# Three small moves in the middle of a hybrid attention layer: a k copy on ScalarE, two key norms, and one step of a GELU given to GpSimd

## The chip, the cores and the metric

The kernel runs on one core of a Trainium2 chip. The metric is the device time of one execution in microseconds (us), the median of several runs. TensorE does the matmuls, VectorE (DVE), ScalarE (ACT) and GpSimd (POOL) the work on tiles, and DMA queues the traffic with the chip's memory.

## The reference, cut to what matters

```python
h = rms_norm(x, norm_w)                      # x: 512 tokens of 1024
q_a, k_a, v_a, z_a, q_b, kc, vc, ksl, vsl, kwn, vwn, gate_b, z_b, gate_m = split(h @ w_in)
# mixer A: 8 heads of 64, causal attention over blocks of 256 keys
o_a = moba(rms_norm(heads(q_a)), rms_norm(heads(k_a)), heads(v_a), bias_a)
# mixer B: a compressed, a selected and a window branch
k_cmp = rms_norm(compress(kc)); v_cmp = compress(vc)     # compress: gelu(win @ w1) @ w2
o_b = nsa(rms_norm(heads(q_b)), k_cmp, v_cmp, rms_norm(ksl), vsl, rms_norm(kwn), vwn, gate_b, bias_b)
merged = sigmoid(g1) * ((o_a * silu(z_a)) @ w_a) + sigmoid(g2) * ((o_b * silu(z_b)) @ w_b)
out = x + merged @ w_out
```

All numbers are float32. With 512 tokens the block choices of both mixers take in every past block, so the attention is dense and causal.

## The kernel before, in words

**Precision.** A float32 matmul is done as three faster ones: each operand is split into a high part (`wh`, `hh`, `ks`) and a low part (`wl`, `hl`, `kx`), and high by high, high by low and low by high are summed in PSUM (`mm3`, L375 to L389). Weights come by DMA in 128x512 tiles `wr`; the high part is a cast on ScalarE or GpSimd (L352, L356), the low part a subtraction on VectorE or GpSimd (L361).

**Order.** Everything is written by Python generators: the projections (`gemms`), the attention units (`attention`), the two compressions (`cmp`). A planner in the kernel keeps an estimated clock `now` and an estimated end of work for each engine (`free`), draws the next piece of matmul work, and runs chains of small operations (`Chain`, L171 to L250) from a heap ordered by estimated time. A step of a chain names the engines that may do it, with a cost; the planner takes the engine that would be done first. What comes out is a fixed order of instructions on each engine. An engine works through its own order strictly, so an instruction that waits holds up those behind it. `Chain(t).call(fn)` runs `fn` when the planner's clock reaches `t`, and costs the planner nothing.

**Attention.** An attention unit is one head. Its scores come in four blocks of 128 queries, the longest first: `sps` = q by `ks` (L1033) and by `kx` (L1034), then on VectorE `sb` (scores and bias, L1052), on ScalarE the exponential `P` (L1067), on VectorE the reciprocal of the sum `sst` (L1070), on GpSimd the scaling of `P` (L1071). One unit later TensorE transposes `P` into `pt` (L1080), ScalarE and VectorE split it into `ph` (L1092) and `pl` (L1094), and TensorE multiplies by v into `O` (L1114). The first transposes of a unit need all four blocks of `P`, the 128x128 one being scaled last.

**k of mixer A** (`k_pair`, L978). Two heads are transposed at once into `pq` (L956). For each, ScalarE casts the high part twice, into the upper and the lower 64 partitions of `ks` (L987); VectorE writes the low part into the upper 64 partitions of `kx` (L989); ScalarE copies that into the lower 64 (L992), after the low parts of both heads. The matmul with `kx` needs both halves.

**k of mixer B** (`norm`, L714, called for the four token tiles of `kb` with `gi` 4). ScalarE takes the projection out of PSUM into `nraw` (L723) and squares it (L725); VectorE sums the squares into `nss` (L726) and scales the sum (L426); GpSimd raises it to the power -1/2, `nr` (L427); two products on VectorE or GpSimd follow (L728, L734). The tiles are read far later, when mixer B's heads begin. The norms of `qb` run through the same function.

**Compression** (`compress_h`, L855), once for k and once for v. After the first matrix `hps` and a small sum `pu` (L878) comes the GELU: ScalarE makes the square and a copy `u` (L885, L886), GpSimd two steps on `gt` (L888, L889), ScalarE the tanh (L890), VectorE the last step (L891: `gt` = (`gt` + 1) by `u`). For k, TensorE goes on with `pk` (L905); for v, VectorE first spreads `gt` into `Gv` (L896).

Of the kernel before, what the change touches and what calls it, by code (L numbers as in the profile page):

```python
# [25 lines left out]
EPS = 1e-6  # L26
# [80 lines left out]
def hybrid_kernel(ctx: ExitStack, tc: tile.TileContext, x, x0, xT, wtok, wchan, wz, wgate, gains, w1,  # L107
                  relone, wbr, wout, consts, out):
    nc = tc.nc
# [19 lines left out]
    now = [0.0]  # L129
# [267 lines left out]
    mhalf = cp.tile([P, 8], F32, name="mhalf")  # L397
# [6 lines left out]
    gn = cp.tile([P, 6, DH], F32, name="gn")  # L404
# [16 lines left out]
    pos = cview("pos").rearrange("p (k i) -> p k i", k=2)  # L421
    w2t = cview("w2").rearrange("p (k a d) -> p k a d", k=2, a=2)

    def rsqrt_mean(c, dst, ss, n, w, parts=P):
        v = (lambda z: z() if callable(z) else z)
        c.do({"D": 70}, lambda e: e.tensor_scalar(v(ss), v(ss), 1.0 / n, EPS, op0=ALU.mult, op1=ALU.add))  # L426
        c.do({"p": 430 + POWC * w}, lambda e: e.tensor_tensor(v(dst), v(ss), mhalf[:parts, :w], op=ALU.pow))  # L427

    def att(name, dt=F32R):
        return ap_.tile([P, 512], dt, name=nm(name), tag="a")  # L430
# [283 lines left out]
    def norm(ch, dst, ps, t, H, gi):  # L714

        b, n = {}, H * DH
        out = dst.bitcast(F32)[:, :n].rearrange("p (h d) -> p h d", d=DH)

        def f0(e):
            b["t"] = alloc("nraw", "nraw", (P, 8, DH))  # L720
            b["raw"] = b["t"][:, :H]
            b["ss"], b["r"] = (sp.tile([P, 8], F32, name=nm(z), tag=z, bufs=4)[:, :H] for z in ("nss", "nr"))
            e.activation(b["raw"], ps[:, :n].rearrange("p (h d) -> p h d", d=DH), AF.Copy, scale=rx[:, t:t + 1])  # L723
        ch.do({"A": 100 + cap(n)}, f0, ps, "nraw")
        ch.do({"A": ca(n)}, lambda e: e.activation(out, b["raw"], AF.Square))  # L725
        ch.do({"D": cd(n)}, lambda e: e.reduce_sum(b["ss"], out, axis=AX.X))  # L726
        rsqrt_mean(ch, lambda: b["r"], lambda: b["ss"], DH, H)
        ch.do(either(n), lambda e: e.tensor_mul(out, b["raw"], b["r"].unsqueeze(2).to_broadcast([P, H, DH])), lambda: b["t"])  # L728
        if gi == 1:
            z = out[:, 4:]  # L730
            ch.do(either(256), lambda e: e.tensor_mul(z, z, gn[:, 1, :].unsqueeze(1).to_broadcast([P, 4, DH])))
        elif gi:
            z = out.rearrange("p (a b) d -> p a b d", a=2)
            ch.do(either(256), lambda e: e.tensor_mul(z, z, gn[:, gi:gi + 2, :].unsqueeze(2).to_broadcast([P, 2, 2, DH])))  # L734

    def hl4(t):
        return t.rearrange("p (h s d) -> p h s d", s=2, d=DH)
# [117 lines left out]
    def compress_h(kv):  # L855
        yield need(f"xw{kv}")
        st = xws[kv]
        yield room("t")
        hps = psum("t", "hps")
        for q in range(8):  # L860
            ws = W1.take(1, 256)
            if W1.i == 1:
                W1.bufs, W.bufs = W1B, NRAW - W1B
            for i in range(2):
                yield ws[i][2].ready
                c = 2 * q + i
# [12 lines left out]
        yield 300
        t1 = sp.tile([P, P], F32, name=nm("gt"), tag="c2")  # L880
        u = sp.tile([P, P], F32, name=nm("u"), tag="u", bufs=1)
        ch = Chain(now[0] + 230)

        def square(e):
            e.activation(t1, ub[:, :P], AF.Square)  # L885
            e.copy(u, ub[:, :P])  # L886
        ch.do({"A": 160}, square)
        ch.do({"D": 200}, lambda e: nc.gpsimd.tensor_scalar(t1, t1, 0.044715, 1.0, op0=ALU.mult, op1=ALU.add))  # L888
        ch.do({"D": 200}, lambda e: nc.gpsimd.tensor_mul(t1, t1, u))  # L889
        ch.do({"A": 200}, lambda e: e.activation(t1, t1, AF.Tanh, scale=0.7978845608028654))  # L890
        ch.do({"D": 200}, lambda e: e.scalar_tensor_tensor(t1, t1, 1.0, u, op0=ALU.add, op1=ALU.mult), ub)  # L891
        G = t1
        if kv:
            yield room("gmt")
            G = alloc("gmt", "Gv", (P, 4, 4, C32))
            ch.do({"D": 600}, lambda e: e.tensor_copy(  # L896
                G, t1.rearrange("p (q c) -> p q c", c=C32).unsqueeze(2).to_broadcast([P, 4, 4, C32])))
        yield ch.ready
        yield from (compress_v2 if kv else compress_k2)(G)
# [75 lines left out]
                 pt if r else None)  # L975
            box.append((z, c))

    def k_pair(boxes, name, col, firsts=None):  # L978

        yield room("t")  # L980
        pt = turn(name, col)
        yield 4 * 109
        c = Chain(now[0] + 230)
        kk = [(att("ks"), att("kx")) for _ in range(2)]
        for r, (ks, kx) in enumerate(kk):
            for i in range(2):
                c.do({"A": 478}, lambda e, r=r, z=ks[64 * i:64 * i + 64, :]: e.copy(z, pt[64 * r:64 * r + 64, :]))  # L987
        for r, (ks, kx) in enumerate(kk):
            c.do({"D": 602}, lambda e, r=r, ks=ks, kx=kx: e.tensor_sub(  # L989
                kx[0:64, :], pt[64 * r:64 * r + 64, :], ks[0:64, :].bitcast(F32)), pt if r else None)  # L990
        for r, (ks, kx) in enumerate(kk):
            c.do({"A": ca(512)}, lambda e, kx=kx: e.copy(kx[64:128, :], kx[0:64, :].bitcast(F32)))  # L992
# [850 lines left out]
```

## Time and profile before

| | us |
|---|---|
| runs shown | 450.40, 452.17, 452.28 |
| their median | 452.17 |
| the profiled execution | 451.19 |
| its span, first to last instruction | 449.4 |
| TensorE busy in the span | 442.5 (98%) |
| VectorE busy | 381.7 (85%) |
| ScalarE busy | 302.9 (67%) |
| GpSimd busy | 202.6 (45%) |

The profiled execution is one of its own, 0.98 below the median of the runs; 1.8 of its time lie outside the span. The granted TensorE clock is 1.0 throughout. A row of the timeline has the start in us, the duration in us, the engine, the line, the operation and its tiles; in brackets stands the idle time of the engine before it and who ended it. `x3` is three equal instructions in a row.

### The profile page before, as it was taken

To read this page: it belongs to the slowest core of one execution; us is meant where nothing else is said; L and a number is where in the kernel's file an instruction comes from. 1 tells how busy PE (TensorE), PEld (TensorE's weight loads), DVE (VectorE), ACT (ScalarE), POOL (GpSimd) and SP (SyncE) were. 2 spreads that over 40 slices of the span, in tenths; PEclk is the share of its full clock that TensorE was granted. 3 is DMA by queue.
4 is the path that set the end of the run, shared out by engine and by line. 5 is a ranking of instruction groups with operands and counts; after the bars stand their busy time and mean duration, and the time that the engine had idled before them with its cause. 6 is when DMAs were issued, how large, how long until landed. Compare 5 with 4: busy or idle time off the path is not lost.

```text
span 449.4 us, 8537 instructions
## 1 busy us (share of the span) xinstructions
PE 442.5 (98%) x2779; PEld 395.2 (88%) x2779; DVE 381.7 (85%) x934; ACT 302.9 (67%) x713; POOL 202.6 (45%) x238
## 2 busy tenths in 40 slices
PE   8999999999999999999999999999999999999997
PEld 7888888899788998888999999989988999998886
DVE  5999899789997797788899999877967699999783
ACT  6866778867988797476878677687764355454460
POOL 1243337866784573176675554764760221311000
PEclk9999999999999999999999999999999999999999
DMA  7885746877975979959978867976667888889872
GB/s 254 293 274 187 243 146 201 212 220 185 272 196 161 220 220 249 298 146 226 278 200 223 212 175 185 253 203 157 196 182 171 230 244 235 258 232 290 279 240 95
DMA packets 55085, 98.21 MB, mean 219 GB/s; under 512 B 5312, under 2 KB 9536, under 8 KB 55040
## 3 DMA queue, kind: packets, MB, share of 16 engines
q1 hardware_dynamic: 39808, 68.30, 47.5%
q0 software_dynamic: 7616, 14.68, 20.1%
q10 hardware_dynamic: 7616, 14.68, 9.9%
q8 instruction: 22, 0.36, 0.3%
q14 instruction: 23, 0.19, 0.1%
HBM read 90.69 MB, written 36.31 MB: 283 GB/s over the span
## 4 chain that ended last, share of the span: by engine, by line
PE 80%; DVE 9%; ACT 5%; DMA 3%; issue 2%; SPq 0%; ACTq 0%; DVEq 0%
PE pgw L386 17%; PE pgt L386 14%; PE pbr L386 10%; PE po L386 9%; PE pgc L386 7%; PE O L1114 5%; PE pgf L680 5%; PE pt L1080 5%; PE sps L1033 3%; PE sps L1034 3%; DMA T<-rtab 1%; DMA wr<-in_w 1%; ACT ks L987 1%; DVE sb L1052 1%; DVE pl L1094 1%
## 5 line engine op out<-in xcount | busy, mean ns | idle before, releaser
L361 DVE TENSOR_TENSOR wl<-wr,wh 128x512 fp32r<-128x512 f32 (+1 forms) x150 | 101.9, 696 | 2.7 <-ACT wh L352 2.1
L352 ACT CAST wh<-wr 128x512 fp32r<-128x512 f32 (+1 forms) x130 | 77.0, 608 | 16.2 <-DMA wr<-wsum 5.4
L356 POOL TENSOR_SCALAR wh<-wr 128x512 fp32r<-128x512 f32 (+1 forms) x39 | 31.5, 819 | 78.4 <-DVE wl L361 24.3
L1071 POOL TENSOR_SCALAR P<-P,sst,gate 128x512 f32<-128x512 f32 (+3 forms) x56 | 46.3, 830 | 40.0 <-DVE sst L1070 32.0
L1067 ACT ACTIVATE P<-sb,sst 128x512 f32<-128x512 f32 (+3 forms) x88 | 50.8, 577 | 16.5 <-DVE sst L1052 15.2
L1052 DVE CUSTOM_DVE_ANT_0 sb<-sps,T 128x512 f32<-128x512 f32 (+3 forms) x96 | 46.0, 483 | 15.3 <-PE sps L1034 13.0
L386 PE MATMUL pgt<-wh,hh 128*128 128x512 f32 (+2 forms) x160 | 56.6, 354 | 0.0
L386 PE MATMUL pgt<-wl,hh 128*128 128x512 f32 (+2 forms) x160 | 55.8, 348 | 0.0
L386 PE MATMUL pgt<-wh,hl 128*128 128x512 f32 (+2 forms) x160 | 55.7, 348 | 0.0
L386 PE MATMUL pgw<-th,wh 128*128 128x256 f32 x240 | 48.9, 281 | 0.4 <-DVE gm L1528 0.4
L1092 ACT CAST ph<-pt 128x512 fp32r<-128x512 f32 (+2 forms) x72 | 33.8, 476 | 19.7 <-PE pt L1080 18.4
L386 PE MATMUL pgw<-hh,wh 128*128 128x256 f32 x160 | 45.2, 282 | 0.3 <-ACT c L1469 0.2
L386 PE MATMUL pgw<-hh,wl 128*128 128x256 f32 x160 | 44.4, 278 | 0.0
L386 PE MATMUL pgw<-hl,wh 128*128 128x256 f32 x160 | 44.4, 277 | 0.0
L1080 PE MATMUL pt<-cst,P 128*128 128x128 f32 x232 | 40.7, 272 | 0.4 <-DVE pl L1094 0.3
L386 PEld LDWEIGHTS pgw<-th,wh 128*128 128x128 f32 x240 | 39.4, 188 | 1.2 <-DVE gm L1528 0.8
L1094 DVE TENSOR_TENSOR pl<-pt,ph 128x512 fp32r<-128x512 f32 (+2 forms) x72 | 38.6, 548 | 1.6 <-ACT ph L1092 1.3
L427 POOL TENSOR_TENSOR nr<-nss,mhalf 128x8 f32<-128x8 f32 (+1 forms) x16 | 26.9, 1680 | 20.5 <-DVE nss L426 18.8
L386 PEld LDWEIGHTS pgt<-wl,hh 128*128 128x128 f32 x160 | 30.1, 188 | 4.1 <-DVE wl L361 0.2
L386 PE MATMUL pgw<-th,wl 128*128 128x256 f32 x120 | 33.3, 277 | 0.0
L386 PEld LDWEIGHTS pgt<-wh,hh 128*128 128x128 f32 x160 | 30.1, 188 | 3.4 <-ACT nraw L723 0.2
L386 PEld LDWEIGHTS pgt<-wh,hl 128*128 128x128 f32 x160 | 30.1, 188 | 3.2
(272 smaller groups left out, 1292.3 us busy)
## 6 DMA issues: line engine op xcount, KB each, us to landing
wr<-wsum SPq DMA_DIRECT2D x56, 256.0 KB, 4.0
wr<-in_wtok SPq DMA_DIRECT2D x36, 256.0 KB, 4.9
wsum<-in_wgate ACTq DMA_DIRECT2D x16, 512.0 KB, 5.0
wsum<-wsum POOLq DMA_DIRECT2D x14, 512.0 KB, 7.5
wr<-in_wgate SPq DMA_DIRECT2D x24, 256.0 KB, 4.7
xsum<-th SPq DMA_DIRECT2D x16, 256.0 KB, 2.6
T<-rtab SPq DMA_DIRECT2D x16, 256.0 KB, 5.3
wr<-in_w SPq DMA_DIRECT2D x16, 256.0 KB, 3.8
```

The costliest lines, as they stand in the source:

```text
L352: e.copy(hi, raw)
L356: e.tensor_scalar(hi, raw, 1.0, 1.0, op0=ALU.mult, op1=ALU.mult)
L361: c.do({"D": cd(n)} if lead else either(n), lambda e, hi=hi, lo=lo, raw=raw: e.tensor_sub(lo, raw, hi.bitcast(F32))).mark((w, 1, i))
L386: nc.tensor.matmul(dst, sts[i][a], mvs[i][b], start=(start and i == a == b == 0), stop=(stop and i == n - 1 and b == 1), skip_group_check= ...
L427: c.do({"p": 430 + POWC * w}, lambda e: e.tensor_tensor(v(dst), v(ss), mhalf[:parts, :w], op=ALU.pow))
L680: nc.tensor.matmul(ps[t][:, :n], (hl if a else hh)[:, k, t * P:(t + 1) * P], w[b], start=(k == a == b == 0), stop=(k == KT - 1 and b == 1))
L1052: e.tensor_tensor_reduce(z["sb"][:, :L], sps[:, :L], T[:, S - L:], scale=-1.0, scalar=3e38, op0=ALU.add, op1=ALU.min, accum_out=st[:, 0, b ...
L1067: e.activation(pv(), z["sb"][:, :L], AF.Exp, bias=st[:, 0, b:b + 1], scale=-1.0, accum_out=st[:, 1, b:b + 1])
L1071: c.do({"P": 315 + 0.834 * L}, lambda e: e.tensor_scalar(pv(), pv(), st[:, 2, b:b + 1], g, op0=ALU.mult, op1=ALU.mult))
L1080: nc.tensor.transpose(pt[:, (b - kb) * P:(b - kb + 1) * P], u.p0 if u.p0 is not None and b == 0 else u.pb[:, POFF[b] + kb * P:POFF[b] + (k ...
L1092: e.copy(z["w"][0], pt[:, :w])
L1094: ch.do({"D": cd(w)}, lambda e: e.tensor_sub(z["w"][1], pt[:, :w], z["w"][0].bitcast(F32)), pt)
```

## The change

One edit in each of three places. In `k_pair`, with `sooner` (set for the pair of heads 4 and 5 of mixer A alone), the copy of the first head's low part into the lower 64 partitions is called as soon as the first subtraction is written (`KX0` = 0), and no longer after the second. In `norm`, for `kb` and token tiles 2 and 3 alone, the steps after the square are each written 2500 ns of the planner's clock later (`KB0`); the planner's own estimates, and with them the choice of engines, stay as they were. In `compress_h`, the last step is two GpSimd instructions, `gt` = `gt` by `u` and `gt` = `gt` + `u`, in place of one on VectorE; the planner still books it on VectorE. This holds for k and v.

```diff
+KX0 = 0
+KB0 = 2500
...
     def norm(ch, dst, ps, t, H, gi):
+        late = (lambda fn: lambda e: Chain(now[0] + KB0).call(lambda: fn(e))) if gi == 4 and t >= 2 else lambda fn: fn
...
-        ch.do({"D": cd(n)}, lambda e: e.reduce_sum(b["ss"], out, axis=AX.X))
-        rsqrt_mean(ch, lambda: b["r"], lambda: b["ss"], DH, H)
+        ch.do({"D": cd(n)}, late(lambda e: e.reduce_sum(b["ss"], out, axis=AX.X)))
+        rsqrt_mean(ch, lambda: b["r"], lambda: b["ss"], DH, H, late=late)
...
-        ch.do({"D": 200}, lambda e: e.scalar_tensor_tensor(t1, t1, 1.0, u, op0=ALU.add, op1=ALU.mult), ub)
+
+        def last(e):
+            nc.gpsimd.tensor_mul(t1, t1, u)
+            nc.gpsimd.tensor_add(t1, t1, u)
+        ch.do({"D": 200}, last, ub)
...
+        def double():
+            nc.scalar.copy(kk[0][1][64:128, :], kk[0][1][0:64, :].bitcast(F32))
+
+        def low(e, r, ks, kx):
+            e.tensor_sub(kx[0:64, :], pt[64 * r:64 * r + 64, :], ks[0:64, :].bitcast(F32))
+            if sooner and not r:
+                Chain(now[0] + KX0).call(double)
...
-                    yield from k_pair(ks, f"qk{h // 4}", 256 + h % 4 * DH)
+                    yield from k_pair(ks, f"qk{h // 4}", 256 + h % 4 * DH, sooner=h == 4)
```

The two products of the norm (L728 and L734 of before) go through `late` in the same way. TensorE's order and that of the DMA queue on SP are the same in both kernels. Line numbers grow by 2 to 15.

On ScalarE, where the pair of heads 4 and 5 is made: `kx_1607` is the low part of head 4, `kx_1609` that of head 5, `nraw` and `kb` belong to the last token tile, `gt` and `u` to the compression of k, `wh` are weight casts. Before:

```order
L723 ACTIVATE nraw_1697<-pgt_1614,rx 128x256
L352 CAST wh_1707<-wr_1601 128x512
L885 ACTIVATE gt_1705<-pu_1701 128x128
L886 COPY u_1706<-pu_1701 128x128
L725 ACTIVATE kb_1672<-nraw_1697 128x256
L352 CAST wh_1718<-wr_1649 128x512
L992 CAST kx_1607<-kx_1607 64x512
L992 CAST kx_1609<-kx_1609 64x512
```

Now:

```order
L726 ACTIVATE nraw_1695<-pgt_1614,rx 128x256
L994 CAST kx_1607<-kx_1607 64x512
L354 CAST wh_1706<-wr_1601 128x512
L888 ACTIVATE gt_1704<-pu_1700 128x128
L889 COPY u_1705<-pu_1700 128x128
L728 ACTIVATE kb_1672<-nraw_1695 128x256
L354 CAST wh_1716<-wr_1649 128x512
L1006 CAST kx_1609<-kx_1609 64x512
```

Head 4's copy has gone ahead of two weight casts and three small instructions; head 5's stands where it stood.

On VectorE, in the same stretch: `nss_1639` and `kb_1613` belong to token tile 2, `nss_1698` (now `nss_1696`) to tile 3, `sb` are the scores of head 4 with 512 and 384 keys. Before:

```order
L989 TENSOR_TENSOR kx_1609<-pq_1586,ks_1608 64x512
L726 TENSOR_REDUCE nss_1698<-kb_1672 128x4
L728 TENSOR_TENSOR kb_1613<-nraw_1638,nr_1640 128x256
L426 TENSOR_SCALAR nss_1698<-nss_1698 128x4
L361 TENSOR_TENSOR wl_1719<-wr_1649,wh_1718 128x512
L734 TENSOR_TENSOR kb_1613<-kb_1613,gn 128x256
L891 SCALAR_TENSOR_TENSOR gt_1705<-gt_1705,u_1706 128x128
L1052 ISA sb_1752,sst_1744<-sps_1739,T_1610 128x512
L1052 ISA sst_1744 128x1
L361 TENSOR_TENSOR wl_1708<-wr_1601,wh_1707 128x512
L1052 ISA sb_1767,sst_1744<-sps_1756,T_1610 128x384
```

Now:

```order
L997 TENSOR_TENSOR kx_1609<-pq_1586,ks_1608 64x512
L729 TENSOR_REDUCE nss_1639<-kb_1613 128x4
L428 TENSOR_SCALAR nss_1639<-nss_1639 128x4
L363 TENSOR_TENSOR wl_1717<-wr_1649,wh_1716 128x512
L1066 ISA sb_1748,sst_1740<-sps_1734,T_1610 128x512
L1066 ISA sst_1740 128x1
L729 TENSOR_REDUCE nss_1696<-kb_1672 128x4
L363 TENSOR_TENSOR wl_1707<-wr_1601,wh_1706 128x512
L1066 ISA sb_1764,sst_1740<-sps_1753,T_1610 128x384
L1066 ISA sst_1740 128x1
L731 TENSOR_TENSOR kb_1613<-nraw_1638,nr_1640 128x256
L1108 TENSOR_TENSOR pl_1758<-pt_1741,ph_1757 128x512
```

Ahead of head 4's first `sb` the two products of tile 2 and the last step of the GELU are gone. Behind it stand, one after the other between the scores and the `pl`, the sum of tile 3, the first product of tile 2 (last but one above), and beyond this piece the scaling of tile 3's sum (behind the `pl` of 512) and the second product of tile 2, ahead of the reciprocals of head 4.

On GpSimd, from there to head 4's `P` (`P_1612`); `nr_1640` is tile 2, `nr_1699` (now `nr_1697`) and `kb_1672` tile 3, `gt` the compression of k. Before:

```order
L427 TENSOR_TENSOR nr_1640<-nss_1639,mhalf 128x4
L888 TENSOR_SCALAR gt_1705<-gt_1705 128x128
L889 TENSOR_TENSOR gt_1705<-gt_1705,u_1706 128x128
L427 TENSOR_TENSOR nr_1699<-nss_1698,mhalf 128x4
L728 TENSOR_TENSOR kb_1672<-nraw_1697,nr_1699 128x256
L734 TENSOR_TENSOR kb_1672<-kb_1672,gn 128x256
L1071 TENSOR_SCALAR P_1612<-P_1612,sst_1744 128x512
L1071 TENSOR_SCALAR P_1612<-P_1612,sst_1744 128x384
L1071 TENSOR_SCALAR P_1612<-P_1612,sst_1744 128x256
L356 TENSOR_SCALAR wh_1839<-wr_1688 128x512
```

Now:

```order
L891 TENSOR_SCALAR gt_1704<-gt_1704 128x128
L892 TENSOR_TENSOR gt_1704<-gt_1704,u_1705 128x128
L429 TENSOR_TENSOR nr_1640<-nss_1639,mhalf 128x4
L896 TENSOR_TENSOR gt_1704<-gt_1704,u_1705 128x128
L897 TENSOR_TENSOR gt_1704<-gt_1704,u_1705 128x128
L429 TENSOR_TENSOR nr_1697<-nss_1696,mhalf 128x4
L1085 TENSOR_SCALAR P_1612<-P_1612,sst_1740 128x512
L731 TENSOR_TENSOR kb_1672<-nraw_1695,nr_1697 128x256
L1085 TENSOR_SCALAR P_1612<-P_1612,sst_1740 128x384
L1085 TENSOR_SCALAR P_1612<-P_1612,sst_1740 128x256
L737 TENSOR_TENSOR kb_1672<-kb_1672,gn 128x256
L358 TENSOR_SCALAR wh_1840<-wr_1687 128x512
```

The power of tile 3 now stands directly ahead of the first `P` of head 4, and both products of tile 3 stand between that and the weight cast; behind the cast the order is the same as before, with head 4's last `P`, the 128x128 one, four places further on. On the v side of the compression GpSimd has the two new instructions behind L889, and VectorE has one less.

More of the change, by code (lines that the diff above doesn't have):

```diff
@@ L422, in hybrid_kernel, with rsqrt_mean @@
     w2t = cview("w2").rearrange("p (k a d) -> p k a d", k=2, a=2)
-    def rsqrt_mean(c, dst, ss, n, w, parts=P):
+    def rsqrt_mean(c, dst, ss, n, w, parts=P, late=lambda fn: fn):
         v = (lambda z: z() if callable(z) else z)
-        c.do({"D": 70}, lambda e: e.tensor_scalar(v(ss), v(ss), 1.0 / n, EPS, op0=ALU.mult, op1=ALU.add))
-        c.do({"p": 430 + POWC * w}, lambda e: e.tensor_tensor(v(dst), v(ss), mhalf[:parts, :w], op=ALU.pow))
+        c.do({"D": 70}, late(lambda e: e.tensor_scalar(v(ss), v(ss), 1.0 / n, EPS, op0=ALU.mult, op1=ALU.add)))
+        c.do({"p": 430 + POWC * w}, late(lambda e: e.tensor_tensor(v(dst), v(ss), mhalf[:parts, :w], op=ALU.pow)))
     def att(name, dt=F32R):
@@ L725, in norm @@
         ch.do({"A": ca(n)}, lambda e: e.activation(out, b["raw"], AF.Square))
-        ch.do({"D": cd(n)}, lambda e: e.reduce_sum(b["ss"], out, axis=AX.X))
-        rsqrt_mean(ch, lambda: b["r"], lambda: b["ss"], DH, H)
-        ch.do(either(n), lambda e: e.tensor_mul(out, b["raw"], b["r"].unsqueeze(2).to_broadcast([P, H, DH])), lambda: b["t"])
+        ch.do({"D": cd(n)}, late(lambda e: e.reduce_sum(b["ss"], out, axis=AX.X)))
+        rsqrt_mean(ch, lambda: b["r"], lambda: b["ss"], DH, H, late=late)
+        ch.do(either(n), late(lambda e: e.tensor_mul(out, b["raw"], b["r"].unsqueeze(2).to_broadcast([P, H, DH]))), lambda: b["t"])
         if gi == 1:
@@ L733, in norm @@
             z = out.rearrange("p (a b) d -> p a b d", a=2)
-            ch.do(either(256), lambda e: e.tensor_mul(z, z, gn[:, gi:gi + 2, :].unsqueeze(2).to_broadcast([P, 2, 2, DH])))
+            ch.do(either(256), late(lambda e: e.tensor_mul(z, z, gn[:, gi:gi + 2, :].unsqueeze(2).to_broadcast([P, 2, 2, DH]))))
     def hl4(t):
@@ L976, in q_pair, with k_pair @@
             box.append((z, c))
-    def k_pair(boxes, name, col, firsts=None):
+    def k_pair(boxes, name, col, firsts=None, sooner=False):
         yield room("t")
@@ L988, in k_pair @@
         for r, (ks, kx) in enumerate(kk):
-            c.do({"D": 602}, lambda e, r=r, ks=ks, kx=kx: e.tensor_sub(
-                kx[0:64, :], pt[64 * r:64 * r + 64, :], ks[0:64, :].bitcast(F32)), pt if r else None)
+            c.do({"D": 602}, lambda e, r=r, ks=ks, kx=kx: low(e, r, ks, kx), pt if r else None)
         for r, (ks, kx) in enumerate(kk):
-            c.do({"A": ca(512)}, lambda e, kx=kx: e.copy(kx[64:128, :], kx[0:64, :].bitcast(F32)))
+            c.do({"A": ca(512)}, lambda e, r=r, kx=kx: (r or not sooner) and e.copy(kx[64:128, :], kx[0:64, :].bitcast(F32)))
             for i, z in enumerate((ks, kx) if firsts else ()):
```

## The prediction, made before the run

> **What bounds the kernel now.** I read the page first, then TensorE's waits, then the timelines of the four engines between 113 and 155 us, where all of the change but one step lies.
>
> ```profile
> PE 442.5 (98%) x2779; PEld 395.2 (88%) x2779; DVE 381.7 (85%) x934; ACT 302.9 (67%) x713; POOL 202.6 (45%) x238
> ```
>
> TensorE is busy for 98% of the span: 6.9 us are all it ever stands, so no change of order can bring more than that. Among TensorE's waits, one stands out:
>
> ```profile
> PE sps L1034 <- ACT kx L992: 1.1, 1, 1.1
> ```
>
> This is the first score matmul of head 4 with the low part of k. TensorE's timeline shows the place, and four later places that I need:
>
> ```profile
> 120.97 0.40 PE L1033 MATMUL sps<-ks,qs 128*128 128x512 f32 x1
> 122.49 0.50 PE L1034 MATMUL sps<-kx,qs 128*128 128x512 f32 x1 [1.12 <-ACT kx L992]
> ...
> 124.40 0.39 PE L1033 MATMUL sps<-ks,qs 128*128 128x256 f32 x1
> ...
> 130.21 0.60 PE L956 MATMUL pq<-cst,qk 128*128 128x128 f32 x4
> ...
> 134.33 0.60 PE L1080 MATMUL pt<-cst,P 128*128 128x128 f32 x4
> ```
>
> The 1.12 in brackets is TensorE standing idle. The matmul before it needs only the high part; this one waits for ScalarE, whose rows just ahead of it are:
>
> ```profile
> 121.16 0.63 ACT L352 CAST wh<-wr 128x512 fp32r<-128x512 f32 x1
> 121.82 1.14 ACT L992 CAST kx<-kx 64x512 fp32r<-64x512 f32 x2
> ```
>
> The two copies of 0.57 follow directly on the cast; ScalarE was simply full. Every other wait of TensorE in this stretch is hidden, which does not say by how much. That has to be taken from the rows of those it waits for.
>
> **The copy sooner.** It removes nothing and moves one copy of 0.57 ahead of two weight casts and three small instructions. The copy now follows the `nraw` of tile 3; its input, the low part of head 4, is written by then. So the second score matmul follows the first at once: 1.12 gained, the idle time itself. What moved behind the copy comes 0.57 later, the cast at 121.16 among them, which now ends at 121.16 + 0.63 + 0.57 = 122.36. VectorE's subtraction of that tile stands in front of head 4's scores:
>
> ```profile
> 121.32 0.42 DVE L726 TENSOR_REDUCE nss<-kb 128x4 f32<-128x256 f32 x1
> 121.66 0.42 DVE L728 TENSOR_TENSOR kb<-nraw,nr 128x256 f32<-128x256 f32 x1
> 121.99 0.42 DVE L426 TENSOR_SCALAR nss<-nss 128x4 f32<-128x4 f32 x1
> 122.33 0.68 DVE L361 TENSOR_TENSOR wl<-wr,wh 128x512 fp32r<-128x512 f32 x1
> 122.93 0.41 DVE L734 TENSOR_TENSOR kb<-kb,gn 128x256 f32<-128x256 f32 x1
> 123.32 0.29 DVE L891 SCALAR_TENSOR_TENSOR gt<-gt,u 128x128 f32<-128x128 f32 x1
> 123.65 0.69 DVE L1052 CUSTOM_DVE_ANT_0 sb<-sps,T 128x512 f32<-128x512 f32 x1
> ...
> 125.51 1.15 DVE L1094 TENSOR_TENSOR pl<-pt,ph 128x512 fp32r<-128x512 f32 x2
> ...
> 126.91 0.21 DVE L1070 RECIPROCAL sst<-sst 128x1 f32<-128x1 f32 x2
> ...
> 129.07 0.41 DVE L1094 TENSOR_TENSOR pl<-pt,ph 128x256 fp32r<-128x256 f32 x1
> ```
>
> Rows on VectorE follow each other without a gap here: from one start to the next a sum takes 0.34, a product 0.33, the scaling 0.34, the subtraction 0.60, the second product 0.39.
>
> **The norms later, as VectorE feels them.** Everything that stood ahead of the subtraction at 122.33 could have gone earlier, but the cast of 122.36 now sets it, so it stays where it was. The product at 122.93 and the GELU step at 123.32 are gone from in front of `sb`, so `sb` starts at about 122.96, 0.69 sooner. It ends at 122.96 + 0.69 = 123.65. The scores with 256 keys, at 124.40 on TensorE, reuse the PSUM bank that this `sb` reads (there are two). TensorE would be there at 124.40 - 1.12 = 123.28 and waits until 123.65 or a little more: about 0.4 of the gain is given back, 0.7 is left.
>
> The work has not gone, though; it stands behind. Between that `sb` and the reciprocals VectorE now has the sum of tile 3 (0.34), the first product of tile 2 (0.33), the scaling (0 to 0.34: a 128x4 instruction, whose 0.34 may be a wait) and the second product (0.39). That is 1.06 to 1.40 against a lead of 0.69, so the reciprocals come 0.4 to 0.7 later, and so does the `pl` of 129.07, which then ends at 129.9 to 130.2. The transposes of q (`pq`, 130.21) need its PSUM buffer; TensorE, 0.7 ahead, would be there at 129.5. It gives back 0.4 to 0.7. **By 130.2 the lead is 0 to 0.3.**
>
> **The norms later and the GELU step, as GpSimd feels them.** This is where I expect the price.
>
> ```profile
> 122.49 1.38 POOL L427 TENSOR_TENSOR nr<-nss,mhalf 128x4 f32<-128x4 f32 x1
> 123.95 0.61 POOL L728 TENSOR_TENSOR kb<-nraw,nr 128x256 f32<-128x256 f32 x1
> 124.64 1.07 POOL L734 TENSOR_TENSOR kb<-kb,gn 128x256 f32<-128x256 f32 x1
> 127.16 1.71 POOL L1071 TENSOR_SCALAR P<-P,sst 128x512 f32<-128x512 f32 x3 [1.46 <-DVE sst L1070]
> 128.85 0.61 POOL L356 TENSOR_SCALAR wh<-wr 128x512 fp32r<-128x512 f32 x1
> 129.41 0.94 POOL L585 DMA_DIRECT2D wsum<-in_wgate  x1
> 130.12 1.95 POOL L427 TENSOR_TENSOR nr<-nss,mhalf 128x8 f32<-128x8 f32 x1
> 131.78 0.81 POOL L427 TENSOR_TENSOR kr<-kss,mhalf 64x1 f32<-64x1 f32 x1
> 132.31 1.12 POOL L1071 TENSOR_SCALAR P<-P,sst 128x128 f32<-128x128 f32 x1
> 133.19 1.50 POOL L361 TENSOR_TENSOR wl<-wr,wh 128x512 fp32r<-128x512 f32 x1
> ```
>
> The 1.46 in brackets is the hole into which the norm of tile 3 fitted. From 127.16 on GpSimd has no hole until head 4's last `P` ends, at 132.31 + 1.12 = 133.43. The four transposes at 134.33 need that `P`: the slack is 0.90. Now the power of tile 3 (1.38) waits for the scaling on VectorE, which stands behind the `pl` of 512. That `pl` stays at about 125.5 (0.69 sooner, less 0.34 and 0.33) and takes about half of the 1.15, so the scaling is done at 126.2 to 126.5 and the power at 127.6 to 127.9. The first `P` stands behind it and starts 0.4 to 0.7 later than 127.16; its reciprocals, at 127.3 to 127.6, are no longer what it waits for. The two products of tile 3 now lie between the first `P` and the last one: 0.61 + 1.07 = 1.7, or 1.2 if the second is as short as the first. So the last `P` ends 1.6 to 2.4 later, at 135.0 to 135.8, and the transposes start 0.7 to 1.5 later than before. The first part of the range is small because the slack of 0.90 is used up, not because little moves. Queued behind the products are also the DMA of 0.94 and the weight cast: VectorE's subtraction of that tile stands behind the cast and holds up the second halves of q, but head 4's transposes come first.
>
> The two GELU instructions themselves (the step before them is one of 0.54, so up to 1.1) run on GpSimd while it would wait for the scaling anyway, and `pk` on TensorE comes more than 1 us after. They cost nothing there. On the v side the cover is this:
>
> ```profile
> 178.86 0.42 DVE L896 COPY Gv<-gt 128x512 f32<-128x512 f32 x1
> ```
>
> ```profile
> 180.71 0.92 PE pv L935 x8
> ```
>
> TensorE needs `Gv` at 180.71; it was ready at 179.28. Up to 1.1 in place of 0.29 makes it 0.8 later, inside the slack of 1.43. Without that cover it would cost at most 0.8.
>
> How long a `P` of 128x128 takes is the widest unknown:
>
> ```profile
> 113.54 1.88 POOL L1071 TENSOR_SCALAR P<-P,sst 128x128 f32<-128x128 f32 x1 [3.62 <-DVE sst L1070]
> ...
> 154.03 0.37 POOL L1071 TENSOR_SCALAR P<-P,sst 128x128 f32<-128x128 f32 x1 [0.79 <-DVE sst L1070]
> ```
>
> The same work took 0.37, 1.12 and 1.88. I keep 1.12, since VectorE is as full there as before; with 0.37 the transposes come 0 to 0.8 later, with 1.88 1.5 to 2.3 later. The Trainium skill, page "SBUF — State Buffer", section "SBUF: two separate sides", says that VectorE (with two SBUF inputs) and GpSimd share a pair of ports as an exclusive lock for a whole instruction, the loser waiting. The 1.12 agrees with it, being near 0.37 and one subtraction of 0.68; by that rule the sum would be about 0.4 where VectorE happens to stand, and 2 or more where it takes the lock twice.
>
> **The sum.** Gain 1.1; given back to VectorE's `sb` and `pl` 0.8 to 1.1; then GpSimd's `P` sets TensorE to 0.7 to 1.5 later than before, of which I take 1.2, above the middle, since the second product was 1.07 beside a busy VectorE. After that TensorE is full and nothing in its waits is long enough to make it good. The profiled execution of 451.19 becomes 452.4. The three runs are 450.40, 452.17 and 452.28, their median 0.98 above the profiled one; the mean of all four is 451.5, and I set the forecast on that: 451.5 + 1.2 = **452.7 us**.
>
> **The rivals.** *The gain stays.* If GpSimd is fast (a last `P` of 0.37, products of 0.61) and VectorE's extra work falls into holes, the 1.1 is kept: 450.4. For it speaks that the wait is plainly there; against it that VectorE has no hole from 121 to 128 and GpSimd none from 127 to 133. *It cancels.* With the short `P` and the lower ends above, TensorE is within 0.5 of where it was: 451.5. It is likely if VectorE, standing behind GpSimd's cast, leaves GpSimd undisturbed. *GpSimd is held up further.* The place is the same chain, the mechanism that VectorE and GpSimd keep each other out: the last `P` takes 1.88 and ends near 136.6, and the two GELU instructions push VectorE's next subtraction by up to 0.54. From 136.6 on (134.33 and 2.3) the kernel is slower by more than 0.5%; the price is 1.5 + 0.76 + 0.5 = 2.8, thus 454.3. The row of 113.54 speaks for it; that such a row stands once against 0.37 and 1.12 speaks against. By the lock of the Trainium skill this is the one that comes out when both engines are full.
>
> **How the numbers follow.** My forecast has 0.55, cancelling 0.22, the gain staying 0.09, GpSimd held up 0.14. One measurement scatters by about 0.9 either way (450.40 to 452.28). The range reaches from the gain staying, with scatter in its favour cut off, to the dearest case: 450.7 to 454.3. About 0.5%, or 2.3 us, is what a measurement of this kernel can tell from no change. Faster by more would need twice the idle time that is removed: 0.03. Slower by more is the held-up case and a little scatter: 0.15. The same: 0.82.
>
> **What would show it.** Right: no wait of 1.1 on `kx` at 121; a new wait of TensorE at the first `pt` of head 4, on GpSimd's `P`, of 0.7 to 1.5; the `P` of 512 at 127.6 to 127.9, the products of tile 3 behind it; VectorE standing 1 us or more behind GpSimd's weight cast near 130. Wrong: that `pt` within 0.3 of 134.33 or earlier, with the last `P` done before 134.3; or a larger wait elsewhere, at `pk` or at `Gv`.

## The result, and the profile after

The changed kernel takes 453.72 us (median of 21 runs, 452.65 to 455.41), the kernel before 451.10 us (21 runs, 450.03 to 454.64). The ratio is 1.0057, 95% interval 1.0042 to 1.0071: slower by 2.6 us (1.9 to 3.2). The forecast of 452.7 was 1.2 us above the level it assumed for the kernel before; the sign was right, the size about half.

First the page's busy times of the changed kernel, whose profiled span is 452.2 us (449.4 before), and the waits of TensorE in it (columns: waiting matmul, releaser, us in total, times, longest):

```profile
PE 443.1 (98%) x2779; PEld 394.0 (87%) x2779; DVE 385.3 (85%) x932; ACT 302.4 (67%) x713; POOL 200.3 (44%) x242
```

```profile
PE sps L1047 <- DVE sst L1066: 1.4, 2, 0.9
PE pw L456 <- POOL ones L402: 0.9, 1, 0.9
PE pt L1094 <- DVE pl L1108: 0.7, 2, 0.4
PE pt L1094 <- POOL P L1085: 0.6, 1, 0.6
```

TensorE stands for 9.1 us in place of 6.9. The wait of 1.1 on `kx` is gone; in the stretch of the change three others are new or longer. TensorE's timeline of the changed kernel shows them one after the other:

```profile
121.40 0.40 PE L1047 MATMUL sps<-ks,qs 128*128 128x512 f32 x1
121.64 0.39 PE L1048 MATMUL sps<-kx,qs 128*128 128x512 f32 x1
...
124.51 0.39 PE L1047 MATMUL sps<-ks,qs 128*128 128x256 f32 x1 [0.93 <-DVE sst L1066]
...
130.70 0.60 PE L963 MATMUL pq<-cst,qk 128*128 128x128 f32 x4
...
135.55 0.66 PE L1094 MATMUL pt<-cst,P 128*128 128x128 f32 x4 [0.56 <-POOL P L1085]
138.09 0.39 PE L1047 MATMUL sps<-ks,qs 128*128 128x256 f32 x1 [0.51 <-DVE sst L1066]
...
141.05 0.41 PE L1094 MATMUL pt<-cst,P 128*128 128x128 f32 x2 [0.39 <-DVE pl L1108]
```

At 121.40 this execution is 0.43 behind the one before (120.97); the change has touched nothing up to there, so the 0.43 is not its work and is taken off below. `kx` comes 0.24 after `ks` (1.52 before), a gain of 1.28. The scores with 256 keys give back 0.93 of it at once. At `pq` TensorE is about level with before (130.70 against 130.21, less 0.43: 0.06 late). At head 4's first `pt` it is 0.79 late (135.55 - 134.33 - 0.43). Then it loses still more. In the kernel before the last two rows stood here:

```profile
136.14 0.28 PE L1033 MATMUL sps<-ks,qs 128*128 128x256 f32 x1
...
138.45 0.38 PE L1080 MATMUL pt<-cst,P 128*128 128x128 f32 x2
```

So TensorE is 1.52 late at head 5's scores with 256 keys, and 2.17 at the `pt` of 141.05. From there to the end the distance stays between 2.0 and 2.4.

VectorE's timeline of the changed kernel, at the two places that matter:

```profile
123.03 0.69 DVE L363 TENSOR_TENSOR wl<-wr,wh 128x512 fp32r<-128x512 f32 x1 [0.87 <-ACT wh L354]
123.75 0.69 DVE L1066 CUSTOM_DVE_ANT_0 sb<-sps,T 128x512 f32<-128x512 f32 x1
...
132.06 0.71 DVE L363 TENSOR_TENSOR wl<-wr,wh 128x512 fp32r<-128x512 f32 x1 [1.25 <-POOL wh L358]
...
135.03 2.27 DVE L363 TENSOR_TENSOR wl<-wr,wh 128x512 fp32r<-128x512 f32 x1
137.33 0.69 DVE L1066 CUSTOM_DVE_ANT_0 sb<-sps,T 128x512 f32<-128x512 f32 x1
```

And the same stretch of the kernel before, VectorE:

```profile
132.47 0.75 DVE L361 TENSOR_TENSOR wl<-wr,wh 128x512 fp32r<-128x512 f32 x1
133.25 0.69 DVE L1052 CUSTOM_DVE_ANT_0 sb<-sps,T 128x512 f32<-128x512 f32 x1
...
133.87 1.39 DVE L728 TENSOR_TENSOR qb<-nraw,nr 128x512 f32<-128x512 f32 x1
```

GpSimd in the changed kernel:

```profile
127.16 1.02 POOL L429 TENSOR_TENSOR nr<-nss,mhalf 128x4 f32<-128x4 f32 x1 [2.12 <-DVE nss L428]
128.46 0.69 POOL L1085 TENSOR_SCALAR P<-P,sst 128x512 f32<-128x512 f32 x1 [0.28 <-DVE gate L757]
129.11 0.61 POOL L731 TENSOR_TENSOR kb<-nraw,nr 128x256 f32<-128x256 f32 x1
129.71 1.04 POOL L1085 TENSOR_SCALAR P<-P,sst 128x384 f32<-128x384 f32 x2
130.71 0.72 POOL L737 TENSOR_TENSOR kb<-kb,gn 128x256 f32<-128x256 f32 x1
131.42 0.61 POOL L358 TENSOR_SCALAR wh<-wr 128x512 fp32r<-128x512 f32 x1
...
134.34 0.81 POOL L429 TENSOR_TENSOR kr<-kss,mhalf 64x1 f32<-64x1 f32 x1
134.88 0.62 POOL L1085 TENSOR_SCALAR P<-P,sst 128x128 f32<-128x128 f32 x1
135.22 1.52 POOL L363 TENSOR_TENSOR wl<-wr,wh 128x512 fp32r<-128x512 f32 x1
```

The power, the `P` of 512, both products of tile 3 and the weight cast stand where they were expected, and VectorE stands 1.25 behind that cast. What was not expected is the row of 2.27. It is VectorE's third `wl` behind the cast, an instruction of 0.7. It ends at 137.30, which is 0.56 after GpSimd's `wl` ends (135.22 + 1.52 = 136.74). In the kernel before, the same pair met the other way round: VectorE's third `wl` took 0.75, GpSimd's `P` of 128x128 beside it 1.12 in place of 0.62, and only the `qb` product behind head 5's first `sb` was held up. That product ends at 135.26 (133.87 + 1.39), again 0.57 after GpSimd's `wl` (133.19 + 1.50 = 134.69). So these instructions of VectorE and GpSimd seem to run one after the other. The Trainium skill, page "SBUF — State Buffer", section "SBUF: two separate sides", says so: VectorE and GpSimd share a pair of ports to SBUF, which is locked for a whole instruction, and the other engine fully blocks. The rows agree (0.56 and 0.57 above). What the change turned over is who blocks: now VectorE, ahead of head 5's `sb`.

In the table, and for the experiments, "TensorE late" is the start of the same TensorE instruction in the kernel less that in the kernel before, taken as the median over a stretch of the kernel before's time, less its value at 119 to 121. "At `pq`" is the stretch 127 to 130, "at `pt`" 134.3 to 136 (head 4's last transposes), "behind" 138.4 to 146. "Third `wl`" is how long VectorE's subtraction took, "`P`" GpSimd's of 128x128. "Measured" is the ratio to the kernel before, timed beside it, as us of 451.

| Kernel | at `pq` | at `pt` | behind | third `wl` | `P` | measured, us (95%) |
|---|---|---|---|---|---|---|
| before | 0 | 0 | 0 | 0.75 | 1.12 | 0 |
| changed | +0.06 | +0.85 | +2.23 | 2.27 | 0.62 | +2.6 (1.9 to 3.2) |
| a_copy | +0.55 | +0.55 | +0.55 | 0.73 | 1.13 | +0.8 (0.0 to 1.6) |
| b_norm | +0.22 | +1.01 | +2.40 | 2.28 | 0.64 | +2.3 (1.5 to 3.2) |
| c_gelu | -0.15 | -0.15 | -0.15 | 0.71 | 1.13 | -0.1 (-0.8 to 0.5) |
| ac | +0.29 | +0.31 | +0.33 | 0.74 | 1.13 | 0.0 (-0.6 to 0.6) |
| tile2_late | -0.32 | +0.07 | +0.88 | 2.28 | 0.62 | +1.2 (0.7 to 1.6) |
| tile3_late | +0.21 | +0.40 | +1.78 | 2.29 | 0.63 | +1.8 (1.1 to 2.5) |
| no_prod3 | +0.09 | +0.09 | +1.02 | 2.32 | 0.64 | +1.0 (0.5 to 1.5) |
| one_input | +0.10 | +0.90 | +1.62 | 1.61 | 0.63 | +1.3 (0.8 to 1.8) |
| sub_on_v | +0.13 | +1.39 | +1.39 | 0.74 | 1.12 | +1.8 (1.1 to 2.6) |
| tile2_products | -0.32 | -0.26 | +0.57 | 2.31 | 0.64 | +1.1 (0.4 to 1.8) |
| tile2_tiny | -0.34 | +0.05 | +0.88 | 1.94 | 0.49 | +4.3 (3.3 to 5.3) |
| after_tiny | +0.08 | +0.88 | +2.28 | 1.94 | 0.49 | +5.0 (4.1 to 5.9) |

But for the last two rows (below), what TensorE has lost by 146 us lies inside the interval of what was measured over the whole kernel: the loss is made in these 25 us. Each trace is one execution of its kernel; that the two engines meet in the same order in every other one is not shown.

### The profile page after: what moved, and what is told of

Its sections match the earlier page's. It is cut to its first block, busy times and chain, and to the rows that moved or that the text cites. A ratio compares the mean times of both kernels' runs of the same rounds, so it can differ in the third digit from the quotient of the medians.

```text
span 452.2 us, 8542 instructions
## 1 busy us (share of the span) xinstructions
PE 443.1 (98%) x2779; PEld 394.0 (87%) x2779; DVE 385.3 (85%) x932; ACT 302.4 (67%) x713; POOL 200.3 (44%) x242
## 4 chain that ended last, share of the span: by engine, by line
PE 73%; DVE 12%; ACT 7%; DMA 3%; issue 3%; POOL 1%; SPq 0%; DVEq 0%; ACTq 0%; POOLq 0%
PE pgw L388 18%; PE pgt L388 11%; PE pbr L388 9%; PE po L388 8%; PE pgc L388 7%; PE O L1128 6%; PE pt L1094 5%; PE sps L1047 3%; PE sps L1048 3%; DVE wl L363 3%; DMA wr<-in_wtok 2%; DMA wr<-in_wgate 2%; DVE sb L1066 1%; DVE pl L1108 1%; ACT ks L1002 1%
## 5 line engine op out<-in xcount | busy, mean ns | idle before, releaser
L363 DVE TENSOR_TENSOR wl<-wr,wh 128x512 fp32r<-128x512 f32 (+1 forms) x150 | 105.0, 718 | 6.4 <-ACT wh L354 4.7
L1085 POOL TENSOR_SCALAR P<-P,sst,gate 128x512 f32<-128x512 f32 (+3 forms) x56 | 45.3, 812 | 40.0 <-DVE sst L1084 31.0
L429 POOL TENSOR_TENSOR nr<-nss,mhalf 128x8 f32<-128x8 f32 (+1 forms) x16 | 25.7, 1607 | 23.4 <-DVE nss L428 22.5
L1094 PEld LDWEIGHTS pt<-cst,P 128*128 128x128 f32 x232 | 28.9, 140 | 5.7 <-POOL P L1085 1.0
```

What stands on the lines that cost most here:

```text
L363: c.do({"D": cd(n)} if lead else either(n), lambda e, hi=hi, lo=lo, raw=raw: e.tensor_sub(lo, raw, hi.bitcast(F32))).mark((w, 1, i))
L429: c.do({"p": 430 + POWC * w}, late(lambda e: e.tensor_tensor(v(dst), v(ss), mhalf[:parts, :w], op=ALU.pow)))
L1085: c.do({"P": 315 + 0.834 * L}, lambda e: e.tensor_scalar(pv(), pv(), st[:, 2, b:b + 1], g, op0=ALU.mult, op1=ALU.mult))
L1094: nc.tensor.transpose(pt[:, (b - kb) * P:(b - kb + 1) * P], u.p0 if u.p0 is not None and b == 0 else u.pb[:, POFF[b] + kb * P:POFF[b] + (k ...
```

## The experiments

**The three parts alone, and two together.** Each takes one or two of the parts back, by these edits of the changed kernel:

```
late = ... if False else lambda fn: fn                       # norms where they were
ch.do({"D": 200}, lambda e: e.scalar_tensor_tensor(...), ub)  # GELU step on VectorE
yield from k_pair(..., sooner=False)                          # copy where it was
```

a_copy (norms and GELU step taken back):

> The sooner copy alone; norms and GELU step as in the kernel before. Theory Q (the loss comes from GpSimd's queue: power and products of tile 3 stand ahead of head 4's P and of a weight cast, and that cast then holds VectorE): the wait of 1.1 on kx goes, but all of it comes back as a wait of about 0.9 to 1.2 at the scores with 256 keys, since VectorE's sb now stands behind a cast that is 0.57 later and the products are still ahead of it; no wait at head 4's first pt; 0 to +0.5 us in all. Rival V (the loss is made in VectorE's own order between head 4's sb and the reciprocals): 0 to +0.5 too. Rival G (the GELU step on GpSimd costs the time and the copy is a plain gain): -0.7 to -1.1 us.

b_norm (copy and GELU step taken back):

> The later norms of mixer B's k alone; copy and GELU step as in the kernel before. Theory Q: the whole loss is here, +1.8 to +2.6 us, with a wait of TensorE at head 4's first pt on GpSimd's P near 135 and VectorE standing 1 us or more behind GpSimd's weight cast near 131. Rival V: +1.0 to +2.6 us, with VectorE late by 1 us or more already at the reciprocals of head 4, before the cast. Rival G: within 0.4 us of the kernel before.

c_gelu (copy and norms taken back):

> The GELU step on GpSimd alone; copy and norms as in the kernel before. Theory Q and rival V: within 0.4 us of the kernel before, the two instructions of about 0.45 lying in time in which GpSimd waits for VectorE, and pk and Gv not waited for. Rival G: +1 to +2.5 us, with a new wait of TensorE at pk or pv, or of VectorE behind them.

ac (norms taken back):

> The sooner copy and the GELU step, without the later norms. Theory Q: 0 to +0.4 us against the kernel before, that is about 2.3 us under the changed kernel; the wait at the scores with 256 keys is 0.3 shorter than with the copy alone, as one VectorE instruction of 0.29 is gone from in front of sb. Rival V: 0 to +0.4 too. Rival G: +1 us or more.

The copy alone: TensorE's timeline has the two score matmuls close together and then the wait, longer than the one removed and than the 0.9 to 1.2 expected:

```profile
120.98 0.40 PE L1047 MATMUL sps<-ks,qs 128*128 128x512 f32 x1
121.21 0.39 PE L1048 MATMUL sps<-kx,qs 128*128 128x512 f32 x1
...
124.86 0.39 PE L1047 MATMUL sps<-ks,qs 128*128 128x256 f32 x1 [1.71 <-DVE sst L1066]
```

The later norms alone (TensorE's timeline of b_norm) show the three waits of the changed kernel with nearly its numbers:

```profile
134.57 0.66 PE L1094 MATMUL pt<-cst,P 128*128 128x128 f32 x4 [0.56 <-POOL P L1085]
137.11 0.39 PE L1047 MATMUL sps<-ks,qs 128*128 128x256 f32 x1 [0.50 <-DVE sst L1066]
140.07 0.41 PE L1094 MATMUL pt<-cst,P 128*128 128x128 f32 x2 [0.40 <-DVE pl L1108]
```

The norms make the loss. The copy is no gain by itself, since what moved behind it holds head 4's `sb`; the GELU step is free. In ac the wait at the scores with 256 keys is 1.53, shorter by 0.18 where 0.3 was expected. Rival G is out: with the copy a plain gain, a_copy would be faster, and c_gelu and ac slower by 1 or more. Theory Q and rival V are not told apart by these four.

**Which tile, and which engine's queue.** tile2_late and tile3_late change one comparison in `norm`; no_prod3 leaves out the two products of tile 3, whose k stays unnormed:

```
late = ... if gi == 4 and t == 2 else lambda fn: fn    # tile2_late (tile3_late: t == 3)
late(lambda e: (gi == 4 and t == 3) or e.tensor_mul(...))   # no_prod3, both products
```

tile2_late:

> The changed kernel with only tile 2's norm of mixer B's k late; tile 3's goes where it went before. Theory Q (GpSimd's queue, which holds tile 3's power and products): 0 to +0.5 us against the kernel before, no wait of 0.5 at head 4's first pt, VectorE not held by the weight cast near 131. Rival V (VectorE's own order between head 4's sb and the reciprocals, to which tile 2's two products belong): +0.8 to +1.5, about half of the loss.

tile3_late:

> The changed kernel with only tile 3's norm late; tile 2's goes where it went before. Theory Q: all of the loss, +1.6 to +2.6 us, with TensorE waiting at head 4's first pt on GpSimd's P and VectorE standing 1 us or more behind the weight cast. Rival V: +0.8 to +1.5, about half of the loss.

no_prod3:

> The changed kernel with the two products of tile 3 in mixer B's k left out (that tile's k stays unnormed), so that GpSimd has two instructions less between head 4's P of 512 and the weight cast; VectorE's order and every other queue stay as in the changed kernel. Theory Q: -0.3 to +0.6 us against the kernel before; the wait at head 4's first pt and VectorE's stand of 1.25 behind the weight cast shrink to 0.3 or less. Rival V: +1.4 to +2.4, as VectorE's order is untouched, and its waits at head 5's sb and pl remain.

Both theories fail in part. Q said that tile 2 costs nothing; it costs 1.2 us, which is in V's range. V said that the products of tile 3 don't matter; without them the wait at head 4's first `pt` and the stand of 1.25 behind the weight cast are gone, as Q had it, and the loss falls from 2.6 to 1.0. What stays in no_prod3 and in tile2_late is the same row. VectorE in no_prod3:

```profile
132.78 2.32 DVE L363 TENSOR_TENSOR wl<-wr,wh 128x512 fp32r<-128x512 f32 x1
```

and in tile2_late, VectorE first, then GpSimd:

```profile
133.00 2.28 DVE L363 TENSOR_TENSOR wl<-wr,wh 128x512 fp32r<-128x512 f32 x1
```

```profile
132.87 0.62 POOL L1085 TENSOR_SCALAR P<-P,sst 128x128 f32<-128x128 f32 x1
133.21 1.51 POOL L363 TENSOR_TENSOR wl<-wr,wh 128x512 fp32r<-128x512 f32 x1
```

133.00 + 2.28 = 135.28 is 0.56 after GpSimd's end at 134.72. Neither kernel has a wait on `P`; both lose what they lose behind head 4's first `pt` (the columns "at `pt`" and "behind"). Nor is it V's mechanism: head 4's first reciprocals start 0.83 late in no_prod3 (127.17 against 126.91, its TensorE being 0.57 early at 119 to 121), and yet TensorE is only 0.09 late at `pt`; in tile3_late they start 0.27 late (126.54, 0.64 early), and the loss is 1.78.

**The two subtractions.** In the changed kernel GpSimd's `wl` of 135.22 is the 57th weight tile's; both runs edit its instruction alone. In one_input it no longer forms the low part; in sub_on_v VectorE does the work:

```
e.tensor_scalar(lo, raw, 1.0, 1.0, ...) if k == 57 else e.tensor_sub(...)    # one_input
(nc.vector if k == 57 else e).tensor_sub(lo, raw, hi.bitcast(F32))           # sub_on_v
```

one_input:

> The changed kernel with GpSimd's subtraction wl of two inputs (1.52 at 135.22) replaced by a multiplication with one input in the same place, so that this weight tile's low part is wrong; all orders stay. Theory L (the two subtractions of two inputs, on VectorE and GpSimd, keep each other out, and this adds to the loss behind head 4's first pt): VectorE's wl of 2.27 takes 0.7, head 5's sb starts 1.4 to 1.6 sooner, the waits of TensorE of 0.51 at head 5's scores with 256 keys and 0.39 at pt go or shrink below 0.2; the loss against the kernel before falls to +0.7 to +1.5 us. Rival S (the stand behind the weight cast alone makes VectorE late, the 2.27 is hidden): within 0.4 us of the changed kernel, +1.9 to +2.8.

sub_on_v:

> The changed kernel with the one subtraction wl that GpSimd does at 135.22 done by VectorE instead, behind kh and ahead of head 5's sb of 384, so that nothing of GpSimd's but the P of 128x128 meets VectorE's third wl. Theory L (behind head 4's first pt the loss is made by VectorE's wl standing still until GpSimd's wl is done): the third wl takes 1.0 (it still waits for P), head 5's first sb starts 1.1 to 1.3 sooner, the wait of 0.51 at head 5's scores with 256 keys goes and the 0.39 at pt shrinks, although VectorE has 0.69 more to do; the wait of 0.56 at head 4's first pt stays; +0.6 to +1.4 us against the kernel before. Rival D (VectorE's being late behind the weight cast is enough, the collision is hidden): +1.9 to +2.8, as VectorE is later still at pl.

In one_input VectorE's and GpSimd's rows are

```profile
134.32 1.61 DVE L370 TENSOR_TENSOR wl<-wr,wh 128x512 fp32r<-128x512 f32 x1
```

```profile
134.17 0.63 POOL L1093 TENSOR_SCALAR P<-P,sst 128x128 f32<-128x128 f32 x1
134.52 0.87 POOL L368 TENSOR_SCALAR wl<-wr 128x512 fp32r<-128x512 f32 x1
```

GpSimd's instruction with one input holds VectorE up as well, so the `wl` did not fall to 0.7. But it is shorter by as much as GpSimd's became shorter (2.27 - 1.61 = 0.66; 1.52 - 0.87 = 0.65), and ends 0.54 after it (135.93 and 135.39). The wait of 0.51 is gone, the 0.39 at `pt` stays; the loss is 1.3, in the range of theory L, outside that of rival S.

In sub_on_v, TensorE, VectorE and GpSimd:

```profile
135.79 0.66 PE L1099 MATMUL pt<-cst,P 128*128 128x128 f32 x4 [1.04 <-POOL P L1090]
```

```profile
131.83 0.69 DVE L367 TENSOR_TENSOR wl<-wr,wh 128x512 fp32r<-128x512 f32 x1 [1.25 <-POOL wh L359]
...
134.78 0.74 DVE L367 TENSOR_TENSOR wl<-wr,wh 128x512 fp32r<-128x512 f32 x1
```

```profile
134.62 1.12 POOL L1090 TENSOR_SCALAR P<-P,sst 128x128 f32<-128x128 f32 x1
```

This is the clearest run. VectorE stands the same 1.25 behind the cast, has one more `wl` of 0.68 to do, and yet nothing is lost behind head 4's first `pt`: +1.39 there and +1.39 at 146. Being late behind the cast is therefore covered; the collision is what TensorE felt there. Rival D falls in the trace. The measured time decides nothing here: 1.8 (1.1 to 2.6) lies above theory L's 1.4 and below rival D's 1.9, and overlaps both. One thing theory L had wrong: here VectorE got the port first, `P` took 1.12, and the wait on it is 1.04 in place of 0.56. The collision is paid on one side or on the other.

**Who gets the port.** Up to then VectorE had lost it in every kernel in which it stood at the weight cast (its first `wl` starts 0.03 behind the cast's end), and won it where it came later (0.08 to 0.16 behind it). Two instructions behind the first `wl` were to make it later:

```
if k == 54:
    for _ in range(2):
        nc.vector.tensor_scalar(tiny, tiny, 1.0, 0.0, op0=ALU.mult, op1=ALU.add)   # tiny: 128x8
```

tile2_tiny:

> tile2_late with two instructions of 128x8 added on VectorE, behind the subtraction that waits for GpSimd's weight cast (some 0.15 us more work there). Theory F (in every run in which VectorE stood at that cast, its third subtraction wl behind it lost the port to GpSimd's last P of head 4 and to GpSimd's own wl, and took 1.6 to 2.3; in every run in which VectorE came 0.08 or more later than the cast it took 0.75 or less and P took 1.1; the loss of tile2_late is this order): with VectorE 0.15 later the third wl takes 0.7 to 0.8 again, P 1.1, head 5's sb starts 1.2 to 1.4 sooner, and the loss of 1.2 us falls to +0.0 to +0.6. Rival D (the loss comes from VectorE being late as such, and the added work can only add): third wl 2.2, +1.2 to +1.6 us.

after_tiny:

> The changed kernel with the same two instructions added. Theory F: third wl 0.7 to 0.8; P of 128x128 takes 1.1 in place of 0.62, so that the wait at head 4's first pt grows from 0.56 to about 1.1; head 5's sb starts 1.2 to 1.4 sooner and the waits of 0.51 and 0.39 behind it go; in all +1.0 to +1.7 us against the kernel before, 0.5 to 1.3 less than the changed kernel. Rival D: +2.4 to +2.9.

Theory F fell. The two instructions took 0.36, not 0.15, and VectorE came too late altogether; in tile2_tiny, VectorE and GpSimd:

```profile
134.80 1.94 DVE L367 TENSOR_TENSOR wl<-wr,wh 128x512 fp32r<-128x512 f32 x1
```

```profile
134.44 0.49 POOL L1095 TENSOR_SCALAR P<-P,sst 128x128 f32<-128x128 f32 x1
134.78 1.40 POOL L367 TENSOR_TENSOR wl<-wr,wh 128x512 fp32r<-128x512 f32 x1
```

`P` was nearly done and GpSimd's `wl` was there first. The loss in this stretch is what it is without the two instructions (0.88 and 0.88; 2.28 and 2.23). And sub_on_v has VectorE standing at the cast and winning, which contradicts F's rule. In all kernels but these two VectorE's third `wl` starts 0.05 to 0.16 before the end of GpSimd's `kr` instruction, so that both seem to wait for that end. By the traces' nanoseconds VectorE was let through where its row starts 0.156 to 0.196 after that of `P`, GpSimd where it starts 0.127 to 0.162 after it (and at 0.36, here). The two ranges overlap: b_norm lost at 0.162, the kernel before won at 0.156. So neither this distance nor F's rule tells who goes first; it stays open.

The large totals of these two runs come from elsewhere, told at the end.

**A version that might beat both.** Only tile 2's two products late; the sum, scaling and power of tile 2 lose their `late`, and `t >= 2` becomes `t == 2`. tile2_products:

> A version that may beat both: copy and GELU step as in the changed kernel, but of the norms only tile 2's two products are late; tile 2's sum, scaling and power and all of tile 3 go where they went before. Head 4's sb no longer stands behind two VectorE instructions, and GpSimd's queue gets nothing new ahead of head 4's P. Theories Q and F: -0.8 to +0.1 us against the kernel before; the wait at head 4's scores with 256 keys is 0.3 to 0.6 shorter than in ac (1.5), and the third wl takes 0.75. Rival V (any work behind head 4's sb delays the reciprocals and is paid there): +0.3 to +1.0.

It is slower by 1.1 (0.4 to 1.8), so the -0.8 to +0.1 of theories Q and F failed. As expected the wait at the scores with 256 keys is shorter than in ac (0.97 against 1.53), and TensorE is 0.3 ahead at `pq` and `pt`. But VectorE's row is again

```profile
132.35 2.31 DVE L363 TENSOR_TENSOR wl<-wr,wh 128x512 fp32r<-128x512 f32 x1
```

and 0.8 is lost behind it. The rest of this trace's loss is one row, a wait at 384 us. Waits of its kind add up to 0.2 in some kernels' profiles and to 0.5 to 1.5 in others'; whether they have to do with the change, no run shows:

```profile
384.20 0.36 PE L388 MATMUL pgw<-hh,wh 128*128 128x256 f32 x1 [1.13 <-ACT c L1483]
```

No kernel of the study is measurably faster than the one before.

## Why the prediction was right and wrong

- *The wait on `kx` goes:* right. The gain was put at the idle time, 1.12; it was 1.28 by the starts.
- *Given back at the 256 scores, 0.4:* too small. It was 0.93. VectorE's subtraction waits for the cast as said, but the cast comes later than reckoned: `sb` ends at 124.44, less 0.43 124.01, where 123.65 was expected. TensorE came to the place at 123.58, less 0.43 123.15, where 123.28 was expected.
- *At `pq` a lead of 0 to 0.3:* 0.06 behind, just outside: the loss at the scores was 0.5 larger and the gain 0.16 larger; between the scores and `pq` 0.41 was given back (0.4 to 0.7 expected). The run with the copy alone shows that the copy by itself keeps nothing of its gain (0.55 late at `pq`); with only tile 2's products moved as well, and the GELU step, 0.32 of it is left there (tile2_products).
- *GpSimd's queue:* right, within 0.15. The `P` of 512, less 0.43, starts at 128.03 (127.6 to 127.9 expected), the products and the cast stand behind it, the last `P` ends at 135.50, less 0.43 135.07 (135.0 to 135.8).
- *The wait at head 4's first `pt`, 0.7 to 1.5 late, 1.2 taken:* right, 0.79 to 0.85, with `P` at 0.62. The wait in the row is 0.56, under the 0.7 that was named as the sign, and the 0.93 at the scores is larger.
- *The GELU step is free:* right, -0.1 (-0.8 to 0.5) by itself, and nothing on the v side.
- **The step that failed** is the end of the sum: "I keep 1.12, since VectorE is as full there as before", and "After that TensorE is full and nothing in its waits is long enough to make it good". The forecast saw that 1.12 fits a `P` that waits for one subtraction of VectorE, and kept it. It did not ask who waits if the `P` is short: at 0.62 it is VectorE. The forecast offered the short `P` only as the cheaper case. Here it is the dearer one: VectorE then stands still through `P` and through GpSimd's `wl`, 1.5 us, ahead of head 5's first `sb`. That `sb` starts at 137.33 in place of 133.25: 3.65 later once 0.43 is taken off. Its cover was 2.2 (133.25 + 0.69 = 133.94; the matmul that waits for it stood at 136.14). So some 1.45 comes through there in place of 0.8 at `pt` (1.52 by TensorE's row), and 0.65 more at `pl`. These 1.38 behind `pt` were left out of the sum. With VectorE first, and GpSimd's `wl` gone from its queue (sub_on_v), the whole is +1.39, close to the 1.2 that was forecast. That 453.72 lies within 450.7 to 454.3 all the same is owed to the width of the range: its upper end was priced for another mechanism.
- *The rival in which GpSimd is held up further* named the mechanism, two engines that keep each other out, and put it on the wrong engine. With 454.3 its price came near the 453.72 by luck, for a reason that the runs do not bear out: head 4's last `P` took 0.49 to 1.13 in all fourteen kernels, never 1.88.

That the loss behind `pt` is this collision is shown by the two runs that change GpSimd's one instruction. That the norms make it is shown by the parts alone. Not shown is why GpSimd comes first in nine of these fourteen kernels and VectorE in five.

## What to carry to other kernels

A duration that is longer than the same instruction elsewhere may be a wait in disguise: before it goes into a sum, ask for whom it waits and what the other one would pay if the order turned over. Where two engines wait for each other's instructions, cost both orders down to the next TensorE instruction that needs either, not only the one that the trace of before happens to show. And a copy moved up on a full engine is worth only what is left after the thing that it pushed back.

## What the runs showed of the hardware that was not expected

VectorE's subtraction of 128x512 with two inputs from SBUF ends 0.54 to 0.56 after GpSimd's `wl` in all nine kernels in which GpSimd goes first, whether that one has two inputs (1.40 to 1.55) or one (0.87). In the five others GpSimd's `P` of 128x128 ends 0.21 to 0.22 after VectorE's subtraction. That is what one expects of an instruction that starts when the other is done, and not of two that slow each other down.

The two kernels with the added instructions have one more tile of 32 bytes in each partition of SBUF, and most of their groups of matmuls that read `hh` or `hl` are about 1% longer (most of the narrower groups of `pgt` 0.5% or less). TensorE falls behind tile2_late before 119 us as well as after 146. Groups of TensorE in tile2_late (mean ns behind the comma):

```profile
L388 PE MATMUL pgt<-wl,hh 128*128 128x512 f32 x96 | 37.6, 392 | 0.1
L388 PE MATMUL pgw<-hl,wh 128*128 128x256 f32 x160 | 44.4, 277 | 0.0
```

and in tile2_tiny:

```profile
L396 PE MATMUL pgt<-wl,hh 128*128 128x512 f32 x96 | 38.0, 396 | 0.0
L396 PE MATMUL pgw<-hl,wh 128*128 128x256 f32 x160 | 45.0, 281 | 0.0
```

The six groups of these two kinds grow by 2.7 us together (113.1 to 114.3, and 134.0 to 135.5), which is most of the 3.1 between the two kernels (4.3 and 1.2); the group `pgw<-th,wh` stays at 281. Whether the extra tile does it, and how, was not tried. For an experiment it means that a scratch tile and its instructions may not be free: the total of such a kernel can't be compared with that of one that lacks them; only the stretch can.
